# Dilated attention: the two key sets of both heads of a pair joined in one pass, statistics moved by small products, keys loaded once, work moved from VectorE to GpSimd

## The chip, the cores and the metric

The kernel runs on one core of a Trainium2 chip. The metric is the device time of one execution in microseconds (us); three executions gave a median of 2361.89 us (2360.36 to 2362.08). The engines are named as in the profile: PE is TensorE (its weight loads are PEld), DVE is VectorE, ACT is ScalarE, POOL is GpSimd, SP is SyncE, which issues nearly all DMAs here. Each engine works through its own instructions in order; a waiting instruction holds up everything behind it on the same engine.

## The reference, cut to what matters

One encoder layer for 1024 sample rows and 256 prompt rows of width 1024: a half-weighted SwiGLU, a mixer (attention for 512 of the columns, a convolution module for the other 512), a second SwiGLU and a final norm. The change lies within the attention, which has 8 heads of 64 columns and mixes three dilations:

```
DILATED_BRANCHES = ((128, 1), (512, 4), (2048, 16))
for window, dilation in DILATED_BRANCHES:
    o, lse = dilated_branch(q, k, v, slopes, dilation, window // (2 * dilation))
w = softmax(stack(lses), axis=0)
o = sum(w[..., None] * stack(outs), axis=0)
```

Each branch is a softmax over a band of keys at a stride, with a bias that falls linearly with distance; the branches are weighted by their softmax denominators. For the 1024 sample rows the kernel sorts the key/query pairs into two key sets: a first set of 8 blocks of 128 queries that lie 4 rows apart (dilations 4 and 16 together), and a second set of 8 blocks of 128 neighbouring queries (dilation 1). Each set gives an unnormalized output, a minimum and a sum per row; joining the two sets is the step that the change rewrites. The 256 prompt rows have one key set and are only normalized.

## The kernel before

In the span of the profile the stages follow each other: the first SwiGLU to about 910 us, the input projection with the convolution running beside it on the other engines to about 1197, attention to about 1357, the output projection, which starts under the last steps of attention and ends near 1475, then the second SwiGLU.

**Attention** (`attn`, L782 on) goes through `seq`, 8 heads of 9 groups, 72 iterations. Groups 0 to 3 are the first key set of the sample rows, group 4 the prompt rows, groups 5 to 8 the second key set. An iteration issues, in this order: `t_group` for the group of 4 iterations ago (four PE transposes of the probabilities, L943, evacuated from PSUM to `pT` by DVE for groups in `DV_G`, L937, by ACT for the others, L939); `qk_group` for its own group (four products of q with the high and low part of k, L861 and L862, then on DVE the bias and the row minimum into `ast`, L866); small steps by `when(lag, group, step)`; `pv_group` for the group of 6 iterations ago (products with v, L971); `exp_group` (ACT's exponential with the row sum into `ast`, L872). Heads work in pairs: both heads of a pair accumulate into the same two outputs, `oa` and `ob`, which are evacuated after the odd head. A scheduler then lays the instructions of each engine out in one fixed order, near to the order of the code.

**Joining** was done once per head, counted from its last group: `merge1` (16 GpSimd copies of 32 partitions, L892) moves the statistics of the first key set to the rows of the second; `merge2` (three small DVE operations, L900 to L902), `merge3` (ACT's exponential, L905) and `merge4` (DVE, L910 to L915) make two factors for each of 1024 rows; `merge5` turns them by a transpose on PE (`psm`, L920), ACT copies them to `asb` (L922), two DMAs write them to DRAM (`fd`, L925) and two DMAs read them back, spread over 64 partitions (`x`, L932). At lag 10 of the odd head `combine1` multiplies both outputs by them on POOL (L1021). At lag 13 `combine2` adds them: POOL writes the rounded sum `hi` (L1030), DVE the exact sum (L1031) and the remainder `lo` (L1032), the parts that the output projection multiplies.

**Other steps.** `load_qk` loads q twice and both parts of k twice (L808, L810), once for each half of the 128 partitions, since q and k are kept doubled; this is issued two heads ahead. `cast_qb` (L815, POOL) makes a reordered copy of q. `prompt_norm` (L882, DVE) scales the probabilities of the prompt rows. `next_tab` changes the bias tables between heads (L831 on DVE, L833 on POOL).

**DMA queue.** All these DMAs are issued by SP in program order, among them `fd`, `x`, the loads of q, k and v for the head two ahead, and near the end the loads of the weights of the output projection (`raw`, L77; split by ACT, L90, and DVE, L91, into `whi` and `wlo`). Issues that a buffer or an earlier DMA holds up delay those behind them. PSUM has four banks that the score products, transposes and `psm` share in turn, and two double banks for `oa`, `ob` and `pso`.

Of the kernel before, what the change touches and what calls it, by code (L numbers as in the profile page):

```python
# [28 lines left out]
NH = 8  # L29
# [3 lines left out]
NEG = -1e30  # L33
NV = 25
BGA, BGQ, BGV = 9, 4.4, 2.2
DV_G = (1, 4, 7)

# [111 lines left out]
class Trunk:  # L149
# [52 lines left out]

    def rstd(self, src, junk, mul):
        nc = self.nc
        st = self.stp.tile([P, 2], F32, name="st", tag="st", bufs=9)
# [576 lines left out]
    def attn(self, qk, pool, rpool, qd, kd, vd, after):  # L782
# [17 lines left out]
        for i, z in enumerate(tab + [half]):  # L800
            nc.sync.dma_start(z, self.a["tab"][i])

        def load_qk(h):
            d = H.setdefault(h, {})
            q, qb, k, d["v"] = bufs[h % 2]
            f = slice(h * HD, (h + 1) * HD)
            for i in range(2):
                nc.sync.dma_start(q[i * HD:(i + 1) * HD].bitcast(F32), qd[i, f, :])  # L808
            for z, o, s in ((0, 0, 0), (0, HD, 0), (1, 0, 1), (1, HD, 1)):
                nc.sync.dma_start(k[z][o:o + HD, :, 16:16 + 256].bitcast(F32), kd[s, f, :].rearrange("f (c i) -> f c i", c=5))  # L810
            d["q"], d["qb"], d["k"] = q, qb, k

        def cast_qb(h):
            q, qb = bufs[h % 2][0:2]
            nc.gpsimd.tensor_copy(qb.rearrange("p (b c j) -> p b c j", b=8, c=4),  # L815
                                  q[:, 0:NS].rearrange("p (c b j) -> p b c j", b=8, c=4).bitcast(F32))
# [18 lines left out]
        def qk_group(h, g):  # L835
            d = H[h]
            if g == 0:
                d["st"] = self.stp.tile([P, 36], F32, name="ast", tag="ast", bufs=3)
# [39 lines left out]
        def prompt_norm(h):  # L878
            d = H[h]
            nc.vector.reciprocal(d["st"][:, 17:21:2], d["st"][:, 17:21:2])  # L880
            for u in (8, 9):
                nc.vector.tensor_scalar(d["P"][u], d["P"][u], d["st"][:, 2 * u + 1:2 * u + 2], None, op0=OP.mult)  # L882

        def merge1(h):
            d = H[h]
            d["X"] = pool.tile([P, 8, 2], F32, name="ax", tag="ax", bufs=2)
            x = d["X"].rearrange("p (h r) s -> p h r s", h=2)
            for c in range(4):  # L890
                for r in range(4):
                    nc.gpsimd.tensor_copy(x[c * 32:(c + 1) * 32, :, r, :],  # L892
                                          d["st"][r * 32:(r + 1) * 32, 4 * c:4 * c + 4].rearrange("p (h s) -> p h s", s=2))

        def merge2(h):
            d = H[h]
            y = d["y"] = pool.tile([P, 4, 8], F32, name="ay", tag="ay", bufs=2)
            z = d["B"] = d["st"][:, 20:36].rearrange("p (b s) -> p b s", s=2)
            v = nc.vector.tensor_tensor
            v(y[:, 3], d["X"][:, :, 0], z[:, :, 0], op=OP.min)  # L900
            v(y[:, 0], y[:, 3], d["X"][:, :, 0], op=OP.subtract)
# [5 lines left out]
        def merge4(h):  # L907
            d = H[h]
            y, v = d["y"], nc.vector.tensor_tensor
            v(y[:, 2], d["X"][:, :, 1], y[:, 0], op=OP.mult)  # L910
            v(y[:, 3], d["B"][:, :, 1], y[:, 1], op=OP.mult)
            v(y[:, 3], y[:, 2], y[:, 3], op=OP.add)
            nc.vector.reciprocal(y[:, 2], y[:, 3])
            for i in range(2):
                v(y[:, i], y[:, i], y[:, 2], op=OP.mult)  # L915

        def merge5(h):
            d = H[h]
            ps = self.bank("psm")
            nc.tensor.transpose(ps[:16, :P], d["y"].rearrange("p i b -> p (i b)")[:, 0:16], self.ident)  # L920
            sb = pool.tile([16, P], F32, name="asb", tag="asb", bufs=2)
            nc.scalar.activation(sb, ps[:16, :P], AF.Copy)  # L922
            fd = self.dp.tile([2, NS], F32, name=f"fd{h}")
            for i in range(2):
                nc.sync.dma_start(fd[i].rearrange("(c b j) -> b c j", c=4, b=8), sb[8 * i:8 * i + 8].rearrange("b (c j) -> b c j", c=4))  # L925
            if h % 2 == 0:
                d["F"] = [self.tmp("x"), self.tmp("x")]
            else:
                d["F"] = H[h - 1]["F"]
            o = (h % 2) * HD  # L930
            for i in range(2):
                nc.sync.dma_start(d["F"][i][o:o + HD, :], fd[i:i + 1, :].to_broadcast([HD, NS]))  # L932
# [90 lines left out]
        def combine2(h):  # L1023
            d = H[h]
            if h % 2:
                ta, tb = d["t"]
                for t in range(2):
                    c = slice(t * 512, (t + 1) * 512)
                    hi, lo = (z[:, h // 2, :] for z in self.hT[t])
                    nc.gpsimd.tensor_tensor(hi, ta[:, c], tb[:, c], op=OP.add)  # L1030
                    nc.vector.tensor_tensor(ta[:, c], ta[:, c], tb[:, c], op=OP.add)  # L1031
# [5 lines left out]
        load_v(0)  # L1037
        load_qk(1)
        load_v(1)
        cast_qb(0)  # L1040
        cast_qb(1)

        def at(i):
            return seq[i] if 0 <= i < len(seq) else (-1, -1)

        for i in range(len(seq) + LAG + LAG2 + 11):
            def when(k, g, f):
                h, gg = at(i - k)
                if gg == g and h >= 0:
                    f(h)  # L1050

            hq, gq = at(i)
            ht, gt = at(i - LAG)
            hv, gv = at(i - LAG - LAG2)
            if ht >= 0:
                t_group(ht, gt)
            when(5, 8, merge5)
            when(3, 8, merge3)
            if hq >= 0:
                qk_group(hq, gq)  # L1060
            when(2, 4, prompt_norm)
            when(1, 8, merge1)
            when(2, 8, merge2)
            when(4, 8, merge4)
# [12 lines left out]
    def w_out(self, S, base, stages, new_hT):  # L1077
# [253 lines left out]
```

## Time and profile before

| | us |
|---|---|
| median of three executions | 2361.89 |
| the profiled execution's own time | 2361.37 |
| its span | 2359.6 |
| PE busy, whole span | 2288.8 (97%) |
| POOL busy, 1200 to 1380 | 82.16 |
| DVE busy, 1200 to 1380 | 124.73 |
| ACT busy, 1200 to 1380 | 123.68 |
| PE busy, 1200 to 1380 | 163.12 |

PE is the engine that nearly never rests; in the 180 us of attention and the start of the output projection it is idle for 16.9 us in all. A row of the windows view gives a stretch of the span, its length, and for each engine its busy time with its number of instructions; then the TensorE clock that was granted as a share of full speed, the busy share of the DMA engines and GB/s. A row of a timeline gives start, duration, engine, line, operation, output and inputs; in brackets stands how long the engine was idle before it, and what ended that.

### The profile page before, as it was taken

Reading aid. Unit: us, or ns where it says so; the run is one execution under the profiler, and the core shown is the slowest. Engines: PE = TensorE matmul, PEld = TensorE weight load, DVE = VectorE, ACT = ScalarE, POOL = GpSimd, SP = SyncE. Lnnn points to the kernel's source line nnn. Section 1 sums busy time; section 2 is a strip of 40 time slices with the busy share of each in tenths; the row PEclk is TensorE's granted clock in tenths of the full one; section 3 lists DMA queues with packets and bytes.
Section 4 is the critical chain, followed back from the end, with each engine's and each line's share of the span. In section 5 each row is a group of like instructions: output and inputs, shape, how many; then the busy total and the mean of one; then the engine's idle time right before and its main releaser. Section 6 shows DMA issues by size and latency. Waiting matters only on the chain.

```text
span 2359.6 us, 30593 instructions
## 1 busy us (share of the span) xinstructions
PE 2288.8 (97%) x11788; PEld 1959.3 (83%) x11788; DVE 1274.9 (54%) x1796; ACT 808.5 (34%) x1530; POOL 670.3 (28%) x702
## 2 busy tenths in 40 slices
PE   7999999999999999999998999999999999999996
PEld 7888888888788887888887878888888888788885
DVE  5844444344554567998466733834344444545457
ACT  5322222223221224664376722322222222312123
POOL 2332232231000034896125443223233232000004
PEclk9999999999999999999999999999999999999998
DMA  5121221213332333331279642122222222523224
GB/s 161 49 76 59 76 69 61 81 63 112 117 101 78 104 108 125 109 104 50 99 162 180 152 132 96 52 79 63 70 72 63 70 76 77 156 74 94 85 81 154
DMA packets 209240, 223.51 MB, mean 95 GB/s; under 512 B 31012, under 2 KB 161060, under 8 KB 209094
## 3 DMA queue, kind: packets, MB, share of 16 engines
q1 hardware_dynamic: 209094, 221.56, 31.7%
q8 instruction: 92, 1.51, 0.3%
q14 instruction: 54, 0.44, 0.1%
HBM read 163.52 MB, written 58.00 MB: 94 GB/s over the span
## 4 chain that ended last, share of the span: by engine, by line
PE 87%; DVE 4%; DMA 3%; issue 2%; POOL 2%; ACT 2%; SPq 0%; POOLq 0%; ACTq 0%; DVEq 0%
PE psAB L198 8%; PE psAB L199 8%; PE psAB L200 8%; PE psd L198 7%; PE psd L200 7%; PE psd L199 7%; PE psR L199 3%; PE psR L198 3%; PE psR L200 3%; PE psC L198 3%; PE psC L199 3%; PE psC L200 3%; PE psqk L198 2%; PE psqk L199 2%; PE psqk L200 2%
## 5 line engine op out<-in xcount | busy, mean ns | idle before, releaser
L115 DVE TENSOR_TENSOR wb<-raw,wb 128x512 fp32r<-128x512 f32 x240 | 169.3, 707 | 207.6 <-ACT wb L114 202.8
L114 ACT ACTIVATE wb<-raw 128x512 fp32r<-128x512 f32 x240 | 150.6, 629 | 331.3 <-PE psAB L200 137.6
L207 POOL TENSOR_SCALAR st<-st 128x1 f32<-128x1 f32 x70 | 40.7, 581 | 633.8 <-ACT tmp L206 359.3
L198 PE MATMUL psd<-wd,ahl 128*128 128x512 f32 x500 | 197.2, 394 | 7.0 <-ACT y L571 2.1
L451 POOL TENSOR_TENSOR ac<-ac,tmp 128x512 f32<-128x512 f32 x40 | 66.5, 1662 | 465.9 <-DVE tmp L447 443.3
L199 PE MATMUL psd<-wd,ahl 128*128 128x512 f32 x500 | 195.3, 391 | 0.0
L200 PE MATMUL psd<-wd,ahl 128*128 128x512 f32 x500 | 195.1, 390 | 0.0
L536 ACT ACTIVATE ahl<-ar 128x512 fp32r<-128x512 f32 (+1 forms) x132 | 72.8, 556 | 346.3 <-PE psd L200 249.9
L199 PE MATMUL psR<-hT2l,wb 128*128 128x256 f32 x640 | 181.1, 283 | 0.0
L200 PE MATMUL psR<-hT2h,wb 128*128 128x256 f32 x640 | 180.7, 282 | 0.0
L198 PE MATMUL psR<-hT2h,wb 128*128 128x256 f32 x640 | 180.6, 282 | 0.0
L114 ACT ACTIVATE wb<-g 128x512 fp32r<-128x512 f32 x80 | 50.6, 632 | 230.1 <-POOL g L136 95.5
L198 PEld LDWEIGHTS psR<-hT2h,wb 128*128 128x128 f32 x640 | 122.2, 191 | 6.2
L198 PE MATMUL psAB<-hT0h,wb 128*128 128x512 f32 x320 | 125.6, 392 | 0.0
L198 PE MATMUL psC<-hT1h,wb 128*128 128x512 f32 x320 | 125.5, 392 | 0.0
L199 PE MATMUL psC<-hT1l,wb 128*128 128x512 f32 x320 | 125.5, 392 | 0.0
L199 PE MATMUL psAB<-hT0l,wb 128*128 128x512 f32 x320 | 125.5, 392 | 0.0
L199 PEld LDWEIGHTS psR<-hT2l,wb 128*128 128x128 f32 x640 | 122.2, 191 | 3.3
L200 PEld LDWEIGHTS psR<-hT2h,wb 128*128 128x128 f32 x640 | 122.2, 191 | 3.1
L200 PE MATMUL psAB<-hT0h,wb 128*128 128x512 f32 x320 | 124.6, 389 | 0.0
L200 PE MATMUL psC<-hT1h,wb 128*128 128x512 f32 x320 | 124.5, 389 | 0.0
L573 DVE TENSOR_TENSOR y<-y,psd 128x1024 f32<-128x1024 f32 x70 | 85.3, 1218 | 71.5 <-PE psd L200 71.5
(388 smaller groups left out, 6279.6 us busy)
## 6 DMA issues: line engine op xcount, KB each, us to landing
raw<-in_ffn_w_gu_dram SPq DMA_DIRECT2D x88, 512.0 KB
ad<-ac SPq DMA_DIRECT2D x88, 256.0 KB
g<-in_ffn_w_down_dram SPq DMA_DIRECT2D x44, 512.0 KB
ar<-ad SPq DMA_DIRECT2D x88, 256.0 KB
raw<-in_w_in_dram SPq DMA_DIRECT2D x20, 512.0 KB
ar<-ad SPq DMA_DIRECT2D x44, 128.0 KB
ad<-x SPq DMA_DIRECT2D x40, 128.0 KB
x2d<-y SPq DMA_DIRECT2D x10, 512.0 KB
```

The source lines that it names most:

```text
L114: nc.scalar.activation(out[:, 0], src, AF.Copy)
L115: nc.vector.tensor_tensor(out[:, 1], src, out[:, 0].bitcast(F32), op=OP.subtract)
L198: mm(out, lh[0], rh[0], start=first, stop=False, skip_group_check=more)
L199: mm(out, lh[0], rh[1], start=False, stop=False, skip_group_check=more)
L200: mm(out, lh[1], rh[0], start=False, stop=last, skip_group_check=more)
L207: nc.gpsimd.tensor_scalar(st[:, 0:1], st[:, 0:1], 1e-6 / (mul * mul), None, op0=OP.add)
L451: nc.gpsimd.tensor_tensor(a1, a1, q, op=OP.mult)
L536: nc.scalar.activation(hl[0], r, AF.Copy)
L573: nc.vector.tensor_tensor(y[b], y[b], o, op=OP.add)
```

## The change

Four things change, all within `attn` but for one pool size (`st`, 9 to 10 buffers):

- **k once.** `load_qk` loads each part of k into partitions 0 to 63 alone; `double_k`, new, copies it to the other 64 on POOL (one instruction for each part and head, 64 partitions of 5x256). It is issued beside `cast_qb`.
- **Joining once per pair.** The statistics of both heads lie in one tile. `merge0`, new, moves those of the first key set by four products with 0/1 matrices (`sel`, built once on POOL) into PSUM (`psx`); `merge1` is now four DVE copies out of PSUM; `merge2` to `merge4` work on 16 columns in place of 8, once for the odd head. `merge5`, at lag 6 in place of 5, transposes once for the pair, and writes 16 small DMAs `fd` of 2x4x32 (four rows of the loop for each head and output) and four DMAs `x`.
- **Work from DVE to GpSimd.** The two scalings of `prompt_norm`, and the exact sum of `combine2`, now one 128x1024 addition after both `hi`.
- **Times.** The remainders `lo` become `combine3`, at lag 17 (13 for the last head). `combine1` comes at lag 11 (10 for the last head) in place of 10, `combine2` at 14 (13) in place of 13. `DV_G` has four groups in place of three, so one more evacuation of nine goes to DVE.

```diff
-DV_G = (1, 4, 7)
+DV_G = (1, 3, 5, 7)
...
+        sel = pool.tile([P, 4, P], F32, name="sel")
+        for r in range(4):
+            nc.gpsimd.tensor_copy(sel[:, r].rearrange("p (c j) -> p c j", c=4),
+                                  self.ident[:, None, r * 32:(r + 1) * 32].to_broadcast([P, 4, 32]))
...
-            for z, o, s in ((0, 0, 0), (0, HD, 0), (1, 0, 1), (1, HD, 1)):
-                nc.sync.dma_start(k[z][o:o + HD, :, 16:16 + 256].bitcast(F32), kd[s, f, :].rearrange("f (c i) -> f c i", c=5))
+            for z in range(2):
+                nc.sync.dma_start(k[z][0:HD, :, 16:16 + 256].bitcast(F32), kd[z, f, :].rearrange("f (c i) -> f c i", c=5))
...
+        def double_k(h):
+            for z in bufs[h % 2][2]:
+                nc.gpsimd.tensor_copy(z[HD:, :, 16:16 + 256], z[0:HD, :, 16:16 + 256].bitcast(F32))
...
-                nc.vector.tensor_scalar(d["P"][u], d["P"][u], d["st"][:, 2 * u + 1:2 * u + 2], None, op0=OP.mult)
+                nc.gpsimd.tensor_scalar(d["P"][u], d["P"][u], d["st"][:, 2 * u + 1:2 * u + 2], None, op0=OP.mult)
...
+        def merge0(h):
+            d = H[h]
+            d["xp"] = self.bank("psx")[:, 0:128]
+            for r in range(4):
+                mm(d["xp"][:, 32 * r:32 * r + 32], sel[:, r], d["st2"][:, :, 0:16], start=True, stop=True)
...
             for c in range(4):
-                for r in range(4):
-                    nc.gpsimd.tensor_copy(x[c * 32:(c + 1) * 32, :, r, :],
-                                          d["st"][r * 32:(r + 1) * 32, 4 * c:4 * c + 4].rearrange("p (h s) -> p h s", s=2))
+                q = slice(c * 32, (c + 1) * 32)
+                nc.vector.tensor_copy(x[q], z[q, c])
...
-            fd = self.dp.tile([2, NS], F32, name=f"fd{h}")
-            for i in range(2):
-                nc.sync.dma_start(fd[i].rearrange("(c b j) -> b c j", c=4, b=8), sb[8 * i:8 * i + 8].rearrange("b (c j) -> b c j", c=4))
...
-            for i in range(2):
-                nc.sync.dma_start(d["F"][i][o:o + HD, :], fd[i:i + 1, :].to_broadcast([HD, NS]))
+            d["F"] = [self.tmp("x"), self.tmp("x")]
+            for e in range(2):
+                fd = self.dp.tile([2, NS], F32, name=f"fd{h}{e}")
+                for i in range(2):
+                    o = fd[i].rearrange("(c h r j) -> r h c j", c=4, h=2, r=4)
+                    for r in range(4):
+                        q = 16 * i + 8 * e + 2 * r
+                        nc.sync.dma_start(o[r], sb[q:q + 2].rearrange("h (c j) -> h c j", c=4))
+                for i in range(2):
+                    nc.sync.dma_start(d["F"][i][e * HD:(e + 1) * HD, :], fd[i:i + 1, :].to_broadcast([HD, NS]))
...
-                    nc.vector.tensor_tensor(ta[:, c], ta[:, c], tb[:, c], op=OP.add)
+                nc.gpsimd.tensor_tensor(ta, ta, tb, op=OP.add)
+
+        def combine3(h):
+            if h % 2:
+                ta, tb = H[h]["t"]
+                for t in range(2):
+                    c = slice(t * 512, (t + 1) * 512)
+                    hi, lo = (z[:, h // 2, :] for z in self.hT[t])
                     nc.vector.tensor_tensor(lo, ta[:, c], hi.bitcast(F32), op=OP.subtract)
...
-            when(5, 8, merge5)
-            when(3, 8, merge3)
+            odd(3, 3, merge0)
+            odd(6, 8, merge5)
+            odd(3, 8, merge3)
...
-            when(8, 8, lambda h: cast_qb(h + 2) if h + 2 < NH else None)
-            when(13, 8, combine2)
+            when(8, 8, lambda h: (double_k(h + 2), cast_qb(h + 2)) if h + 2 < NH else None)
+            late(14, 13, combine2)
+            late(17, 13, combine3)
...
-            when(10, 8, combine1)
+            late(11, 10, combine1)
```

How the order of the instructions moves is shown at three places. First SP's queue during heads 4 and 5, when the factors of heads 2 and 3, the second pair, are written. Before, around head 3's factors (`fd_10308`), up to the loads for head 6 (`q_9258`, `kH_9260` and `kL_9261` are buffers of the even heads; `v_9272` and `v_9262` those of v):

```order
L823 DMA v_9272<-vd 128x2x64
L825 DMA v_9272<-vd 32x9x64
L925 DMA fd_10308<-asb 8x4x32 x2
L825 DMA v_9272<-vd 32x9x64
L932 DMA x<-fd_10308 64x1024 x2
L825 DMA v_9272<-vd 32x9x64 x2
L808 DMA q_9258<-qd 64x1280 x2
L823 DMA v_9262<-vd 128x2x64 x2
L810 DMA kH_9260<-kd 64x5x256 x2
L810 DMA kL_9261<-kd 64x5x256 x2
```

Now, at the same place (`fd_10257` holds head 2's factors, `fd_10268` head 3's):

```order
L813 DMA q_9258<-qd 64x1280 x2
L835 DMA v_9272<-vd 32x9x64 x3
L952 DMA fd_10257<-asb 2x4x32 x8
L954 DMA x<-fd_10257 64x1024
L952 DMA fd_10268<-asb 2x4x32
L954 DMA x<-fd_10257 64x1024
L952 DMA fd_10268<-asb 2x4x32 x7
L954 DMA x<-fd_10268 64x1024
L835 DMA v_9272<-vd 32x9x64
L954 DMA x<-fd_10268 64x1024
L815 DMA kH_9260<-kd 64x5x256
L815 DMA kL_9261<-kd 64x5x256
```

Four DMAs for head 3 (and four more, a head earlier, for head 2) have become twenty in one run for both. The loads of k for head 6 stand behind all twenty; its q now goes ahead of them.

The second place is POOL at the same pair. Before, from the statistics copies of head 4 (`ax_10440`) to those of head 5 (`tmp_10219` and `tmp_10220` are the two outputs of heads 2 and 3, `x` their factors, `g` a bias table):

```order
L892 COPY ax_10440<-ast_10191 32x2x2 x16
L1021 TENSOR_TENSOR tmp_10220<-tmp_10220,x_10071 128x1024
L1021 TENSOR_TENSOR tmp_10219<-tmp_10219,x_10072 128x1024
L833 TENSOR_SCALAR g_9279<-g_9279 128x768
L815 CAST qb0_9259<-q0_9258 128x1024
L1030 TENSOR_TENSOR hT0h_9218<-tmp_10219,tmp_10220 128x512
L1030 TENSOR_TENSOR hT1h_9220<-tmp_10219,tmp_10220 128x512
L892 COPY ax_10686<-ast_10431 32x2x2 x16
```

Now (the outputs are `tmp_10146` and `tmp_10147`):

```order
L825 CAST qb0_9259<-q0_9258 128x1024
L843 TENSOR_SCALAR g_9279<-g_9279 128x768
L1043 TENSOR_TENSOR tmp_10147<-tmp_10147,x_10255 128x1024
L1043 TENSOR_TENSOR tmp_10146<-tmp_10146,x_10256 128x1024
L821 CAST kH0_9260<-kH0_9260 64x5x256
L821 CAST kL0_9261<-kL0_9261 64x5x256
L1052 TENSOR_TENSOR hT0h_9218<-tmp_10146,tmp_10147 128x512
L1052 TENSOR_TENSOR hT1h_9220<-tmp_10146,tmp_10147 128x512
L896 TENSOR_SCALAR pr_10462<-pr_10462,ast_10135 128x256 x2
L1053 TENSOR_TENSOR tmp_10146<-tmp_10146,tmp_10147 128x1024
```

The 16 copies per head are gone; between and behind the multiplications stand the doubling of k for head 6 (L821) and, behind those and the additions, the scaling of head 5's prompt probabilities (L896). In the pair before this one L896 stands ahead of L1052; in the pair after it there is no L821.

The third place is the end of SP's queue in attention, behind the last pair's factors. Before:

```order
L77 DMA raw<-in_w_out_dram 128x1024 x4
L925 DMA fd_11240<-asb 8x4x32 x2
L932 DMA x<-fd_11240 64x1024 x2
L77 DMA raw<-in_ffn_w_gu_dram 128x8x128 x2
L77 DMA raw<-in_w_out_dram 128x1024
```

Now:

```order
L77 DMA raw<-in_w_out_dram 128x1024 x4
L952 DMA fd_11115<-asb 2x4x32 x8
L954 DMA x<-fd_11115 64x1024
L952 DMA fd_11126<-asb 2x4x32
L954 DMA x<-fd_11115 64x1024
L952 DMA fd_11126<-asb 2x4x32 x7
L954 DMA x<-fd_11126 64x1024 x2
L77 DMA raw<-in_ffn_w_gu_dram 128x8x128 x2
L77 DMA raw<-in_w_out_dram 128x1024
```

The last of the eight weight loads of the output projection keeps its place behind the factors, whose DMAs have gone from 4 to 20.

More of the change, by code (lines that the diff above doesn't have):

```diff
@@ L204, in rstd @@
         nc = self.nc
-        st = self.stp.tile([P, 2], F32, name="st", tag="st", bufs=9)
+        st = self.stp.tile([P, 2], F32, name="st", tag="st", bufs=10)
         nc.scalar.activation(junk, src, AF.Square, scale=D ** -0.5 / mul, accum_out=st[:, 0:1])
@@ L837, in qk_group @@
             if g == 0:
-                d["st"] = self.stp.tile([P, 36], F32, name="ast", tag="ast", bufs=3)
+                if h % 2 == 0:
+                    d["st2"] = self.stp.tile([P, 2, 36], F32, name="ast", tag="ast", bufs=2)
+                else:
+                    d["st2"] = H[h - 1]["st2"]
+                d["st"] = d["st2"][:, h % 2]
                 d["P"] = {}
@@ L909, in merge4 @@
             y, v = d["y"], nc.vector.tensor_tensor
-            v(y[:, 2], d["X"][:, :, 1], y[:, 0], op=OP.mult)
-            v(y[:, 3], d["B"][:, :, 1], y[:, 1], op=OP.mult)
+            v(y[:, 2], d["X"][:, :, :, :, 1], y[:, 0], op=OP.mult)
+            v(y[:, 3], d["B"][:, :, :, :, 1], y[:, 1], op=OP.mult)
             v(y[:, 3], y[:, 2], y[:, 3], op=OP.add)
@@ L919, in merge5 @@
             ps = self.bank("psm")
-            nc.tensor.transpose(ps[:16, :P], d["y"].rearrange("p i b -> p (i b)")[:, 0:16], self.ident)
-            sb = pool.tile([16, P], F32, name="asb", tag="asb", bufs=2)
-            nc.scalar.activation(sb, ps[:16, :P], AF.Copy)
-            fd = self.dp.tile([2, NS], F32, name=f"fd{h}")
-            for i in range(2):
[L925 to L930, printed above, removed]
-            for i in range(2):
-                nc.sync.dma_start(d["F"][i][o:o + HD, :], fd[i:i + 1, :].to_broadcast([HD, NS]))
+            nc.tensor.transpose(ps[:32, :P], d["y"].rearrange("p i e r h -> p (i e r h)")[:, 0:32], self.ident)
+            sb = pool.tile([32, P], F32, name="asb", tag="asb", bufs=1)
+            nc.scalar.activation(sb, ps[:32, :P], AF.Copy)
+            d["F"] = [self.tmp("x"), self.tmp("x")]
[8 more added lines that the diff above has]
+                    nc.sync.dma_start(d["F"][i][e * HD:(e + 1) * HD, :], fd[i:i + 1, :].to_broadcast([HD, NS]))
         def evac(g, ps):
@@ L1039, in attn @@
         load_v(1)
+        double_k(0)
         cast_qb(0)
+        double_k(1)
         cast_qb(1)
@@ L1050, in when, with late, odd @@
                     f(h)
+            def late(k, k_last, f):
+                for lag, hs in ((k, range(NH - 1)), (k_last, (NH - 1,))):
+                    h, gg = at(i - lag)
+                    if gg == 8 and h in hs:
+                        f(h)
+            def odd(k, g, f):
+                when(k, g, lambda h: f(h) if h % 2 else None)
             hq, gq = at(i)
@@ L1061, in attn @@
             when(2, 4, prompt_norm)
-            when(1, 8, merge1)
-            when(2, 8, merge2)
-            when(4, 8, merge4)
-            when(8, 8, lambda h: cast_qb(h + 2) if h + 2 < NH else None)
-            when(13, 8, combine2)
+            odd(3, 3, merge1)
+            odd(2, 8, merge2)
+            odd(4, 8, merge4)
+            when(8, 8, lambda h: (double_k(h + 2), cast_qb(h + 2)) if h + 2 < NH else None)
+            late(14, 13, combine2)
+            late(17, 13, combine3)
             if hv >= 0:
```

15 lines of the change are left out of this document (8 added, 7 removed).

## Prediction
> **What bounds the kernel now.** I read the page's busy times first, then the windows by head, then the timelines of PE, DVE and POOL at the places where PE stood still, and last the chain of waits at the end of attention.
>
> ```profile
> span 2359.6 us, 30593 instructions
> PE 2288.8 (97%) x11788; PEld 1959.3 (83%) x11788; DVE 1274.9 (54%) x1796; ACT 808.5 (34%) x1530; POOL 670.3 (28%) x702
> 1200.00:1380.00 180.00, 163.12 (x993) 145.26 (x994) 124.73 (x458) 123.68 (x384) 82.16 (x161) 0.94 0.80 172
> ```
>
> PE is the bound of the whole; the only stage that the change touches leaves PE 16.9 us idle in 180 (last row: PE, PEld, DVE, ACT, POOL). By head, each row from the first score product of one head to that of the next (heads 1, 2, 3, 5, 7, the last cut at its last group):
>
> ```profile
> 1213.93:1232.39 18.46, 16.70 (x119) 15.42 (x118) 12.83 (x58) 13.75 (x48) 7.11 (x19) 1.00 1.02 183
> 1232.39:1248.62 16.23, 16.23 (x117) 15.06 (x115) 11.85 (x54) 14.77 (x48) 6.67 (x18) 1.00 1.00 193
> 1248.62:1272.38 23.76, 18.65 (x114) 17.03 (x112) 13.65 (x54) 12.14 (x40) 14.94 (x22) 0.86 0.87 169
> 1289.96:1310.52 20.56, 17.94 (x114) 16.03 (x112) 15.95 (x54) 12.43 (x41) 12.02 (x22) 0.92 0.83 160
> 1327.80:1346.16 18.36, 16.28 (x105) 14.84 (x104) 14.35 (x53) 11.61 (x41) 11.76 (x21) 0.91 0.39 122
> ```
>
> Head 2 is all PE, 16.23 us, 1.80 for each of 9 groups. Heads 3, 5 and 7, in which the outputs of the pair before are combined, are 7.5, 4.3 and 3.9 us longer (the last against 8 groups, 14.4). In each PE stands once, and then runs at a lower clock for a while (0.86, 0.92 and 0.91 in their rows):
>
> ```profile
> 1216.49 0.39 PE L862 MATMUL pss<-kL,q 128*128 128x256 f32 x1 [1.76 <-DMA kL<-kd]
> 1264.92 0.58 PE L861 MATMUL pss<-kH,qb 128*128 128x256 f32 x1 [5.11 <-DVE ast L866]
> 1293.97 1.91 PE L971 MATMUL op<-pT,v 128*128 128x256 f32 x4 [2.26 <-ACT pT L939]
> 1331.62 2.02 PE L971 MATMUL op<-pT,v 128*128 128x256 f32 x4 [2.08 <-ACT pT L939]
> 1263.40:1270.30 6.90, 5.38 (x19) 4.84 (x20) 6.90 (x24) 4.35 (x14) 4.96 (x17) 0.51 0.63 128
> ```
>
> The first row is head 1's. The last is the 6.9 us behind the gap of head 3: the granted clock is 0.51. The causes stand on DVE and POOL:
>
> ```profile
> 1253.41 4.70 POOL L1021 TENSOR_TENSOR to<-to,x 128x1024 f32<-128x1024 f32 x2 [7.68 <-DMA x<-fd]
> 1262.45 1.73 DVE L1031 TENSOR_TENSOR to<-to 128x512 f32<-128x512 f32 x1 [6.79 <-POOL hT0h L1030]
> 1288.39 4.69 POOL L1021 TENSOR_TENSOR tmp<-tmp,x 128x1024 f32<-128x1024 f32 x2 [5.36 <-issue]
> 1290.83 2.28 DVE L901 TENSOR_TENSOR ay<-ay,ax 128x8 f32<-128x8 f32 x1
> 1328.48 2.28 DVE L901 TENSOR_TENSOR ay<-ay,ax 128x8 f32<-128x8 f32 x1
> ```
>
> In head 3 DVE's exact sum stands in DVE's queue waiting 6.79 us for POOL, with the next row minima behind it. In heads 5 and 7 a DVE operation on 8 columns takes 2.28 us beside POOL's multiplication; ACT's exponential of the joining waits for it, the evacuation of `pT` behind that, and PE for `pT`.
>
> **What the change takes away.** The exact sum leaves DVE, and the joining comes once a pair, after odd heads, while the multiplications come a head later: the three collisions go. I take the excess of the three heads, 7.5 + 4.3 + 3.9 = 15.7 us, and of head 1's wait for `kL` half, 0.8, since k's DMAs are halved but a POOL copy follows. **−16.5 us** (−20 with all of head 1's excess and some more, −10 where half of head 3's excess and a third of the others' stays as a smaller wait).
>
> **What it adds on PE.** Before: one transpose a head. Now, a pair: four products with `sel`, each with a weight load, and one transpose less. No row shows such products; four transposes of 128 columns take 0.44, 0.11 each:
>
> ```profile
> 1219.77 0.44 PE pst L943 x4
> L971 PEld LDWEIGHTS oa<-pT,v 128*128 128x128 f32 x160 | 27.5, 201 | 2.7
> L892 POOL COPY ax<-ast 32x4 f32<-32x4 f32 x128 | 29.7, 232 | 13.7 <-ACT pr L872 8.8
> ```
>
> Eight instructions by 0.11, less 0.11, is 0.77 a pair, **+3.1** for four; from 0 (hidden in what idle time stays) to 6.4 (eight by the 201 ns of a weight load).
>
> **What it adds beside PE.** POOL loses 128 copies (29.7 us, the row above) and gains, by these rows,
>
> ```profile
> L815 POOL CAST qb<-q 128x1024 fp32r<-128x1024 f32 x7 | 7.3, 1037 | 29.8 <-DMA q<-qd 29.8
> L833 POOL TENSOR_SCALAR g<-g 128x768 f32<-128x768 f32 x7 | 15.0, 2137 | 7.4 <-DVE ast L866 7.4
> L1030 POOL TENSOR_TENSOR hT0h<-to 128x512 fp32r<-128x512 f32 x2 | 2.6, 1276 | 0.0
> L937 DVE COPY pT<-pst 128x512 f32<-128x512 f32 x24 | 16.5, 686 | 5.9 <-PE pst L943 5.9
> L882 DVE TENSOR_SCALAR pr<-pr,ast 128x256 f32<-128x256 f32 x16 | 4.9, 348 | 0.0
> ```
>
> 16 doublings of k at 1.3 (1037 ns by 1280 for 1024 elements) = 20.8, 16 scalings at 0.71 (2137 by 256 for 768) = 11.4, and 4 sums at 2.35 (half of 4.70) = 9.4: 12 us more, 94 of 180. DVE loses 4.9 and gains 8 evacuations, 5.5. Both have room in the mean, so their sums cost nothing; what counts is where POOL's queue is late, since scaling and doubling are now waited for by PE.
>
> For that, a table by hand, from the last score product of the odd head (t = 0):
>
> ```profile
> 1309.71 0.36 PE L861 MATMUL pss<-kH,qb 128*128 128x256 f32 x1
> 1320.85 0.63 SPq L925 DMA_DIRECT2D fd<-asb  x2
> 1358.77 0.64 SPq L925 DMA_DIRECT2D fd<-asb  x2
> 1360.33 1.09 SPq L932 DMA_DIRECT2D x<-fd  x2
> 1364.47 4.75 POOL L1021 TENSOR_TENSOR tmp<-tmp,x 128x1024 f32<-128x1024 f32 x2 [23.00 <-DMA x<-fd]
> ```
>
> The first `fd` was issued 11.1 after it (head 5: 1309.71 to 1320.85), now a group later, 12.9. Then SP issues 16 `fd` at 0.32 (5.1), four `x` at 0.55 (2.2), with one landing between, 0.9 (1358.77 + 0.64 to 1360.33), and the last lands 3.05 later (1360.33 + 1.09 to 1364.47): 24.2. POOL: two multiplications, 28.9; in the second pair two doublings of k, 31.5; two `hi`, 34.1; two scalings, 35.5; the sum, 37.9. The transposes that need the scaled prompt group come 18 groups after t = 0, at 32.4: **3.1 late**. DVE's `lo` is in its queue at about 36 there, in head 6's first group, and waits till 37.9; I count 1.5. The doubled k is in time (31.5 for 34.2). In the first pair the scaling stands ahead of `hi`, in the third no k is doubled: 24.2 + 4.7 + 2.6 + 1.4 = 32.9 in both, 0.5 late each, 1.0; and one collision of a small DVE operation with a POOL sum, 2.3 by the 2.28 rows. **+8** (0 to 14).
>
> A row bears on those collisions:
>
> ```profile
> 1293.05 2.13 POOL L833 TENSOR_SCALAR g<-g 128x768 f32<-128x768 f32 x1
> 1293.79 0.15 DVE L910 TENSOR_TENSOR ay<-ax,ay 128x8 f32<-128x8 f32 x1
> ```
>
> POOL's one-input scaling ran over a two-input DVE operation that still took 0.15, so the 2.28 belongs to POOL's two-input operations, which the change has in `hi`, sum and multiplication; the 32 scalings and doublings are left out. The Trainium skill, page "SBUF — State Buffer", section "Who interferes with whom", says that a DVE instruction with two SBUF inputs and any GpSimd instruction that reads SBUF shut each other out. L901 agrees with it, L910 doesn't; by the rule the new one-input instructions would hold DVE too, and the sum be as in the third rival below.
>
> The doublings of heads 0 and 1 fall into the end of the input projection, where POOL is busy 37.3 of 40 us:
>
> ```profile
> 970.00:1010.00 40.00, 40.00 (x200) 34.08 (x199) 36.83 (x36) 24.97 (x46) 37.28 (x38) 1.00 0.51 149
> ```
>
> This is the densest stretch of that stage; q and k of head 0 come at its end, and PE has products of its own till then. **0** (−1 to +4, three of the four doublings ahead of the first score product).
>
> **The end of attention.** There the chain of waits runs through a DMA:
>
> ```profile
> 1362.78 8.62 DMA raw<-in_w_out_dram
> ...
> 1372.51 1.24 DVE wlo L91
> 1373.79 0.50 PE pso L199
> 1346.16:1376.36 30.20, 30.07 (x147) 24.72 (x145) 16.84 (x28) 15.91 (x27) 7.28 (x4) 1.00 0.66 202
> ```
>
> The last weights of the output projection are issued right behind the pair's factors and two other loads, and PE, fully busy until then (30.07 of 30.20), gets them just in time. The 14 more `fd` and two more `x` push this issue back by 14 × 0.32 + 2 × 0.55 = 5.6, and the transpose a group later by about 0.5: PE would stand some 6 us, and the clock drop behind it, as after the other gaps, adds 1.4. **+7.5** (4, if the weights land two or three us sooner, to 9).
>
> **Sum.** −16.5 + 3.1 + 8 + 0 + 7.5 = +2.1 on the profiled execution's own 2361.37 (span 2359.6; the median of the runs is 0.5 above it): **2363.5 us**. The bounds of the terms that most decide, +8 and +7.5, give 2352 to 2371.
>
> **Rivals.** (1) *The new waits stay away.* `fd` may be issued earlier, and PE can go on with other groups when the scaling is late, as no row of before shows PE waiting for POOL directly. Against it: POOL's queue is in order and the table has it 3 us late. With +2 for the waits and +4 at the end: −16.5 + 3.1 + 2 + 4 = −7.4, 2354. (2) *The factors are late in all pairs*, slower. SP's twenty DMAs follow each other in time only if none waits for an earlier one; if one or two landings of up to 3 us come between, with the DMA engines 0.83 to 1.00 busy as in the rows of heads 2, 3 and 5, the factors come 4 us later, at 28.2. POOL's multiplications hold its queue meanwhile, with scaling and doubling behind, and by the table none of the three pairs has slack: 3 × 4 = +12, 2375.5. It decides from factors later than 24 on, by 3 us for each. (3) *POOL still holds DVE*: if its scalings and doublings also shut out DVE's small operations, half of what heads 3, 5 and 7 lost, 8 us, comes back: 2371. The rule of the skill's page above would bring this one about.
>
> **Chances.** Forecast 0.43, of which 0.37 within 0.2%, the rest split; rival 1 0.28; rival 2 0.18; rival 3 0.07; anything else 0.04. About 4.7 us (0.2%) is what a measurement of this kernel can tell from no change. So faster 0.32, same 0.38, slower 0.30. The range goes from just below rival 1 to just above rival 2, 2350 to 2377; the forecast's own is 2356 to 2369.
>
> **What would show it.** Heads 3, 5 and 7 near 17 us, no 2 us DVE operation on 16 columns, and no DVE wait for `hi`: the −16.5. PE waiting for POOL's L896 in head 5: the table. SP's `fd` issues over 0.32 each or `x` landing later than 24 us after the odd head's last product: rival 2. PE idle some 6 us before the last `wlo` at about 1365 to 1372 of the new span: the end. It is wrong if the weights come no later, or if a PE wait for row minima is left in head 3.

## The result, and the profile after

The changed kernel takes **2386.81 us** (median of 5, 2384.58 to 2388.93), the kernel before 2361.89 beside it: a ratio of 1.0115, 95% interval 1.0102 to 1.0129, slower by some 25 us. The forecast was 2363.5, its range 2350 to 2377.

First the page of the changed kernel, its span and busy times:

```profile
span 2387.1 us, 30597 instructions
PE 2311.3 (97%) x11816; PEld 1959.8 (82%) x11816; DVE 1266.8 (53%) x1760; ACT 805.6 (34%) x1514; POOL 693.8 (29%) x614
```

The span is 27.5 us longer, and PE is 22.5 us busier, although only 28 more of its instructions are recorded. Next the windows view: of the kernel before, from the first score product to the last group of head 7, from there to the last product of the output projection, 40 us in the middle of the second down projection, which the change doesn't touch, and heads 4 and 6:

```profile
1197.46:1346.16 148.70, 133.32 (x857) 120.84 (x856) 109.15 (x433) 110.31 (x363) 74.99 (x156) 0.93 0.85 171
1346.16:1473.54 127.38, 124.91 (x587) 103.67 (x586) 49.42 (x60) 41.87 (x74) 44.48 (x49) 0.99 0.36 121
2160.00:2200.00 40.00, 40.00 (x178) 33.14 (x177) 20.78 (x22) 7.88 (x12) 0.00 (x0) 1.00 0.29 90
1272.38:1289.96 17.58, 17.20 (x120) 15.36 (x117) 13.39 (x58) 15.76 (x54) 7.55 (x19) 1.00 0.95 180
1310.52:1327.80 17.28, 17.09 (x120) 15.40 (x117) 13.84 (x58) 15.24 (x53) 7.72 (x19) 1.00 0.90 170
```

and of the changed kernel: attention, its heads 2 to 6, the end of attention with the output projection, and the same 40 us:

```profile
1203.52:1352.50 148.98, 136.12 (x883) 121.74 (x881) 102.35 (x395) 106.56 (x346) 85.73 (x65) 0.94 0.66 139
1239.65:1257.41 17.76, 16.94 (x116) 15.03 (x115) 12.48 (x53) 13.86 (x46) 7.47 (x7) 1.00 0.47 96
1257.41:1275.46 18.05, 17.45 (x124) 15.78 (x122) 11.79 (x48) 13.44 (x43) 12.88 (x9) 1.00 0.85 172
1275.46:1296.30 20.84, 18.52 (x117) 16.27 (x115) 15.12 (x55) 13.59 (x45) 12.21 (x10) 0.92 0.48 90
1296.30:1316.51 20.21, 17.57 (x124) 15.83 (x121) 11.30 (x48) 13.21 (x43) 15.35 (x11) 1.00 0.88 166
1316.51:1336.98 20.47, 18.75 (x116) 16.92 (x115) 15.54 (x55) 13.94 (x45) 9.54 (x7) 0.83 0.27 63
1352.50:1488.19 135.69, 127.16 (x589) 104.10 (x588) 48.13 (x62) 42.15 (x74) 50.50 (x51) 0.99 0.35 116
2160.00:2200.00 40.00, 40.00 (x173) 32.19 (x172) 18.80 (x21) 7.48 (x11) 0.00 (x0) 1.00 0.27 83
```

Four things are to be seen. Attention as a whole is as long as before (148.98 for 148.70): heads 3 and 7 are 5.7 and 2.8 us shorter, but heads 2, 4 and 6 are 1.5 to 3.3 longer. The end of attention with the output projection is 8.3 longer. Attention begins 6.1 us later, and what follows the output projection takes 898.9 in place of 886.1, 12.8 more. So 18.9 us are lost in stages whose code is the same. There, in the last row, PE is busy all the time at full clock, but does 173 products in 40 us where it did 178. The groups of one shape tell which products are slower (mean ns of one after the comma), before:

```profile
L199 PE MATMUL psd<-wd,ahl 128*128 128x512 f32 x500 | 195.3, 391 | 0.0
L198 PE MATMUL psAB<-T2h,wb 128*128 128x512 f32 x160 | 62.3, 389 | 0.0
L199 PE MATMUL psd<-wdh0h,ahl 128*128 128x512 f32 x120 | 46.7, 389 | 0.0
```

and after:

```profile
L199 PE MATMUL psd<-wd,ahl 128*128 128x512 f32 x500 | 198.0, 396 | 0.0
L198 PE MATMUL psAB<-T2h,wb 128*128 128x512 f32 x160 | 63.1, 394 | 0.0
L199 PE MATMUL psd<-wdh0h,ahl 128*128 128x512 f32 x120 | 46.7, 389 | 0.0
```

Products with `wd` and `T2` (and `T3`, `T4`) take 5 ns more each, those with `wdh0h` nothing. `wdh0h` lies in SBUF ahead of the pool of small statistics, whose size the change alters (`st` 9 to 10 buffers, `ast` 3 of 144 bytes to 2 of 288); the others lie behind it (but for four tiles of `wd` at the other end of SBUF), and in the built program they stand 128 bytes higher than before (`T2h` at 125280 in place of 125152 in each partition). 1440 products with T and 1500 with `wd`, at 5 ns, are 15 us of the 18.9. In the trace such a product starts 227 ns after the last one before, 232 after (medians).

Inside attention, the waits of PE in the changed kernel (total, times, longest):

```profile
PE pss L875 <- DVE ast L880: 4.7, 3, 2.2
PE pst L965 <- POOL pr L896: 4.6, 3, 2.6
PE pso L199 <- DVE wlo L91: 4.5, 2, 4.0
PE pso L198 <- DVE tmp L212: 3.1, 1, 3.1
```

The second is the wait for POOL's scaling that the prediction's table had: 2.59 us of it in head 5 and 0.55 in head 3. The remaining 1.43 stands at the end of head 0, before any factors are written, so late factors aren't its cause. For the second pair SP issued the first `fd` 16.5 us after the last group of head 3 began (1274.54), by SP's timeline:

```profile
1291.06 3.60 SPq L952 DMA_DIRECT2D fd<-asb  x8
```

and POOL's timeline from there is:

```profile
1304.03 5.44 POOL L1043 TENSOR_TENSOR tmp<-tmp,x 128x1024 f32<-128x1024 f32 x2 [4.72 <-DMA x<-fd]
1309.53 1.25 POOL L821 CAST kH<-kH 64x1280 fp32r<-64x1280 f32 x1
1310.72 1.25 POOL L821 CAST kL<-kL 64x1280 fp32r<-64x1280 f32 x1
1312.06 1.27 POOL L1052 TENSOR_TENSOR hT0h<-tmp 128x512 fp32r<-128x512 f32 x1
1313.29 1.26 POOL L1052 TENSOR_TENSOR hT1h<-tmp 128x512 fp32r<-128x512 f32 x1
1314.53 1.82 POOL L896 TENSOR_SCALAR pr<-pr,ast 128x256 f32<-128x256 f32 x2
1316.32 2.36 POOL L1053 TENSOR_TENSOR tmp<-tmp 128x1024 f32<-128x1024 f32 x1
1318.62 1.04 POOL L825 CAST qb<-q 128x1024 fp32r<-128x1024 f32 x1
1319.63 2.15 POOL L843 TENSOR_SCALAR g<-g 128x768 f32<-128x768 f32 x1
1321.84 1.25 POOL L821 CAST kH<-kH 64x1280 fp32r<-64x1280 f32 x1
```

DVE's joining of the next pair falls beside the end of this work (DVE's timeline of the same time):

```profile
1317.16 1.56 DVE L922 TENSOR_TENSOR ay<-ax,ast 128x16 f32<-128x16 f32 x1
1318.76 0.94 DVE L923 TENSOR_TENSOR ay<-ay,ax 128x16 f32<-128x16 f32 x1
1319.62 0.17 DVE L924 TENSOR_TENSOR ay<-ay,ast 128x16 f32<-128x16 f32 x1
1322.37 0.75 DVE L934 TENSOR_TENSOR ay<-ay 128x16 f32<-128x16 f32 x1
```

L922 ends as POOL's sum L1053 ends, L923 as the cast of q ends, L934 as the doubling of k ends; L924 takes its 0.17, but it started together with the one-input L843. At the start of head 4 it is POOL's `hi` additions and the cast of q that hold L923 for 1.18 us and L924 for 1.06. L843 holds such an operation too, if only in its first part: at the start of head 2, L923 began 0.11 us into L843 (1240.64) and took 0.76. The kernel before shows the same:

```profile
1277.11 2.13 POOL L833 TENSOR_SCALAR g<-g 128x768 f32<-128x768 f32 x1
1277.27 0.68 DVE L912 TENSOR_TENSOR ay<-ay 128x8 f32<-128x8 f32 x1
```

L912 ended 0.84 us after L833 had begun. In the profiles of all runs, 40 of these small operations began 0.08 to 0.68 us into a 128x768 TENSOR_SCALAR; every one ended 0.84 to 0.89 us after its start, and those that began 0.7 to 2.0 us into it took 0.15 to 0.19.

At the end of attention, DVE's timeline shows a wait that the prediction didn't have:

```profile
1376.42 3.50 DVE L91 TENSOR_TENSOR wlo<-raw,whi 128x1024 fp32r<-128x1024 f32 x3 [12.84 <-DMA fd<-asb]
1386.94 1.28 DVE L91 TENSOR_TENSOR wlo<-raw,whi 128x1024 fp32r<-128x1024 f32 x1 [7.02 <-ACT whi L90]
```

The remainder of the fifth unit of weights is held up for 12.84 us by the DMAs that read `asb`: in the built program its tile (225248 to 229344) takes over the bytes of `asb` (228832), and may be written only when all 16 `fd` have read them.

### The profile page after: what moved, and what is told of

The parts are those of the page before. It is cut to its first block, busy times and chain, and to the rows that moved or that the text cites. A ratio compares the mean times of both kernels' runs of the same rounds, so it can differ in the third digit from the quotient of the medians.

```text
span 2387.1 us, 30597 instructions
## 1 busy us (share of the span) xinstructions
PE 2311.3 (97%) x11816; PEld 1959.8 (82%) x11816; DVE 1266.8 (53%) x1760; ACT 805.6 (34%) x1514; POOL 693.8 (29%) x614
## 4 chain that ended last, share of the span: by engine, by line
PE 84%; DVE 4%; DMA 4%; POOL 3%; issue 2%; ACT 1%; SPq 1%; POOLq 0%; ACTq 0%; DVEq 0%
PE psAB L198 8%; PE psAB L200 8%; PE psAB L199 8%; PE psd L198 7%; PE psd L199 7%; PE psd L200 7%; PE psR L198 3%; PE psR L199 3%; PE psR L200 3%; PE psC L199 3%; PE psC L198 3%; PE psC L200 3%; PE psqk L198 2%; PE psqk L200 2%; PE psqk L199 2%
## 5 line engine op out<-in xcount | busy, mean ns | idle before, releaser
L198 PE MATMUL psd<-wd,ahl 128*128 128x512 f32 x500 | 199.6, 399 | 7.1 <-ACT y L571 2.4
L199 PE MATMUL psd<-wd,ahl 128*128 128x512 f32 x500 | 198.0, 396 | 0.0
L200 PE MATMUL psd<-wd,ahl 128*128 128x512 f32 x500 | 197.9, 396 | 0.0
```

Of the source, the lines that this page charges most:

```text
L198: mm(out, lh[0], rh[0], start=first, stop=False, skip_group_check=more)
L199: mm(out, lh[0], rh[1], start=False, stop=False, skip_group_check=more)
L200: mm(out, lh[1], rh[0], start=False, stop=last, skip_group_check=more)
```

## The experiments

**Is it the place in SBUF? (e1 to e4).** In the kernel before, unused bytes are put into the pool of small statistics (n = 32 floats for e1, 16 for e2), with one `asb` buffer to make room. In the changed kernel the same with n = 32 (e3) and 96 (e4), room being made by one `ay` buffer, in e4 one `ax` buffer too:

```diff
-        self.stp = ctx.enter_context(tc.tile_pool(name="stp", bufs=4))
+        self.stp = ctx.enter_context(tc.tile_pool(name="stp", bufs=4)); self.stp.tile([P, n], F32, name="pad", tag="pad", bufs=1)
```

> The kernel before with 128 unused bytes per partition in the pool of small statistics (and one asb buffer in place of two to make room), so that every SBUF tile allocated behind that pool lies 128 bytes higher, as in the changed kernel. Layout theory: products whose moving operand is T2, T3, T4 or wd go from 227 ns start to start (389 to 393 ns mean length) to about 232 (395), and the time rises by 15 to 20 us, to about 2379. Rival (the slowdown outside attention comes from the changed instructions themselves): these products stay at 227 ns and the time within 5 us of 2362.

> The kernel before with 64 unused bytes in the same pool (asb one buffer). Layout theory with a period above 64 bytes: the same products get slower, by 5 ns each if any address off the old one does it, or stay at 227 ns if only some offsets do; time 2362 to 2380. Rival: 227 ns, within 5 us of 2362.

> The changed kernel with 128 unused bytes in the same pool (and one ay buffer to make room), so that the tiles behind it lie 256 bytes higher than before. Layout theory with a period of 256 bytes: T2, T3, T4 and wd products back at 227 ns, time 15 to 19 us below the changed kernel, 2368 to 2372. Layout theory with a longer period, or the rival: 232 ns and 2387.

> The changed kernel with 384 unused bytes in the same pool (one ay and one ax buffer), tiles 512 bytes higher than before. Layout theory with a period of 256 or 512 bytes: 227 ns and 2368 to 2372. Rival: 232 ns and 2387.

Measured: e1 2380.27 (one run), e2 2370.65 (one run), e3 2371.96 (ratio to before 1.0051, 1.0036 to 1.0066), e4 2370.39 (1.0047, 1.0029 to 1.0066); before, on the same chip, 2359.68. The windows row of e1, with nothing changed but these bytes and the `asb` buffer (e12 below has one `asb` buffer too, and is fast), is that of the changed kernel:

```profile
2160.00:2200.00 40.00, 40.00 (x173) 32.17 (x172) 19.55 (x21) 7.89 (x12) 0.00 (x0) 1.00 0.27 82
```

and that of e4, the changed kernel with 384 more, that of the kernel before:

```profile
2160.00:2200.00 40.00, 40.00 (x178) 33.14 (x177) 20.52 (x22) 7.34 (x12) 0.00 (x0) 1.00 0.29 89
```

Medians from start to start for `T2h`: 232 ns in e1, 231 in e2, 227 in e3 and e4. The layout theory holds, with a period of 256 bytes: 64 and 128 bytes are bad, 256 and 512 good. 64 costs about half as much: of the three products that belong together, the first takes 232 ns there, the second (`T2l`) 226 as before, the third 229, and the time rose by 11 us where it rose by 20.6 in e1. In the changed kernel the layout is worth 2386.8 − 2370.4 = 16 us of the 25. What is left, some 11 us over the kernel before on the same chip, is the change's own doing, and e4 is the base for the next.

**Which of the two operands? (e8, e12).** e8 lowers the other end of SBUF, with the stationary and streamed weights, by 128 bytes; e12 does that and raises all the rest by 128 as well (both with one `asb` buffer):

```diff
+    self.ctx.enter_context(tc.tile_pool(name="padr", bufs=1, side="right")).tile([P, 32], F32, name="padr")
     wp, wp_x = pool_("wp", bufs=9, side="right")
...
+        self.const.tile([P, 32], F32, name="padl")   # e12 only
         self.hp = ctx.enter_context(tc.tile_pool(name="hp", bufs=1))
```

> The kernel before with the tiles of the other end of SBUF (wb, ahl, part of wd, the stationary and streamed weights) 128 bytes lower, and T2 to T4 and hT0 to hT2 where they were. If it is the distance between the moving and the stationary operand that counts: products of T2 to T4 and of hT0 and hT1 with wb go from 227 to 232 ns, time 2380 or more. If it is the place of the moving operand alone: T and hT products stay at 227 ns, only those with wd on that side slow down, time 2362 to 2370.

> The kernel before with both ends of SBUF moved: hT, T and the left part of wd 128 bytes higher (96 in place of 224 modulo 256), wb and ahl 128 bytes lower (also 96 in place of 224). Theory that the distance between moving and stationary operand modulo 256 decides: it is 0 again, products at 226 to 227 ns, time within 5 us of before. Rival (224 is a good place and 96 a bad one, for either operand): 232 ns or more and 2380 or more.

e8: 2389.43 (one run), no faster than the changed kernel; now the products with `wdh0h` are slow as well, though that tile hasn't moved (e8's group):

```profile
L199 PE MATMUL psd<-wdh0h,ahl 128*128 128x512 f32 x120 | 47.3, 394 | 0.0
```

e12: 2356.22 (0.9992, 0.9983 to 1.0002), with `T2h` at 389 ns again. Neither operand's own place counts, but the **distance of the two modulo 256 bytes**: 0 is fast. (All tiles of weights leave the same remainder, so no run tells the weights in use from those that are loaded beside the product.) In the kernel before it happened to be 0 for nearly all products of these stages (T from 125152 and `wb` from 184288 both leave 224).

**What of the change costs the other 11 us? (e5, e6, e7, e9, e13).** All on the base of e4. e5 lays the columns of the factors out by head, set and row, so that one DMA takes 8 rows of `asb`:

```diff
-            y = d["y"] = pool.tile([P, 4, 2, 4, 2], F32, name="ay", tag="ay", bufs=1)
+            d["yr"] = pool.tile([P, 4, 2, 2, 4], F32, name="ay", tag="ay", bufs=1)
+            y = d["y"] = d["yr"].rearrange("p i e h r -> p i e r h")
...
-                    for r in range(4):
-                        q = 16 * i + 8 * e + 2 * r
-                        nc.sync.dma_start(o[r], sb[q:q + 2].rearrange("h (c j) -> h c j", c=4))
+                    q = 16 * i + 8 * e
+                    nc.sync.dma_start(fd[i].rearrange("(c b j) -> b c j", c=4, b=8), sb[q:q + 8].rearrange("b (c j) -> b c j", c=4))
```

e6 puts the scaling of `prompt_norm` back on DVE; e7 takes `double_k` out and loads k by the four DMAs of before; e9 is e5 and e7 together; e13 is e5 with the doubling on ACT:

```diff
-                nc.gpsimd.tensor_scalar(d["P"][u], ...)   # e6
+                nc.vector.tensor_scalar(d["P"][u], ...)
...
-                nc.gpsimd.tensor_copy(z[HD:, :, 16:16 + 256], z[0:HD, :, 16:16 + 256].bitcast(F32))   # e13
+                nc.scalar.activation(z[HD:, :, 16:16 + 256], z[0:HD, :, 16:16 + 256].bitcast(F32), AF.Copy)
```

> The kernel of e4 (changed kernel, tiles 512 bytes higher than before) with the factors laid out so that 4 DMAs fd in place of 16 write them for a pair. Theory: the 12 DMAs less give SP's queue back 12 x 0.3 = 3.7 us for each pair, the last weights of the output projection are issued and PE's wait for wlo (4.2 us in e4) falls to under 1, and the factors reach POOL 3 to 4 us earlier: 4 to 8 us below e4, 2362 to 2366. Rival (the time is lost to POOL's work holding DVE and PE, wherever the DMAs stand): within 2 us of e4's 2370.

> The kernel of e4 with the two scalings of prompt_norm back on DVE. Theory: PE's waits for POOL's scaling (2.9 us in e4) go and POOL is 14 us less busy, so its sums come earlier and collide less with the joining: 3 to 6 us below e4, 2364 to 2367. Rival: DVE pays with 4.9 us of its own and the waits move to the row minima: within 2 us of 2370.

> The kernel of e4 with k loaded in four DMAs a head again and no doubling on POOL. Theory: POOL is 20 us less busy and its sums come 2.5 us earlier in the first two pairs, SP has two DMAs more a head (1.1 us): 1 to 4 us below e4, 2366 to 2369. Rival (loading once pays, since DMA traffic holds the factors up): 1 to 4 us above e4.

> The kernel of e4 with both k in four DMAs (as e7) and the factors in four DMAs (as e5). Theory (the doubling on POOL costs attention 8 us, the 20 DMAs of the factors cost the end 4 us): attention as in e7, 141 us from first to last score product, PE's wait for wlo under 2, time 2 to 5 us below e7: 2358 to 2361, the same as before. Rival (with k's DMAs back SP is late and the factors come no earlier): 2363.

> The kernel of e5 (k loaded once, factors in four DMAs) with the doubling of k on ACT in place of POOL. Theory (the doubling costs because POOL's queue stands for k's DMA and for the 1.25 us of each copy, with the scaling and the sums behind it): most of the 11 us between e5 and e9 comes back, 2357 to 2362. Rival (it costs because k arrives later or because of the reads themselves): within 2 us of e5's 2368. ACT pays 2.5 us a head, and if ACT's queue stands for the DMA in turn, it is slower than e5.

| | us (median) | ratio to before, interval |
|---|---|---|
| e4, base | 2370.39 | 1.0047 (1.0029 to 1.0066) |
| e5, four `fd` | 2367.76 | 1.0039 (1.0026 to 1.0052) |
| e6, scaling on DVE | 2373.11 | 1.0062 (1.0049 to 1.0075) |
| e7, k in four DMAs | 2363.17 | 1.0021 (1.0011 to 1.0031) |
| e9, e5 and e7 | 2356.29 | 0.9992 (0.9982 to 1.0001) |
| e13, e5 with doubling on ACT | 2373.37 | 1.0072 (1.0059 to 1.0086) |

The windows of attention, first score product to head 7's last group, one kernel each: e4, e7, e9.

```profile
1195.86:1344.96 149.10, 136.46 (x882) 121.06 (x881) 105.04 (x395) 106.23 (x346) 85.93 (x65) 0.95 0.64 139
```

```profile
1196.27:1336.93 140.66, 132.32 (x882) 120.27 (x881) 103.18 (x395) 106.50 (x346) 65.43 (x49) 0.96 0.86 179
```

```profile
1194.55:1331.85 137.30, 129.64 (x882) 118.93 (x881) 99.61 (x394) 106.26 (x343) 71.08 (x51) 0.98 0.88 184
```

The runs come from several chips, so the ratios are what can be compared. Loading k once makes attention 8.4 us longer (149.10 for 140.66): the largest single cost within the change. The small DMAs cost less than expected beside it, 2.6 us, which the overlapping intervals of e4 and e5 don't tell from nothing, though PE's longest wait for `wlo` fell from 4.2 to 0.8 us; without the loading once they cost 6.9 (2363.17 to 2356.29). With both undone, attention is 11.4 us shorter than before, so the joining by pairs does there what it was reckoned to do. The whole is no faster all the same. The end of attention with the output projection takes 132.4 us in e9, for 127.4 before:

```profile
1331.85:1464.25 132.40, 126.49 (x587) 103.76 (x588) 53.71 (x63) 42.72 (x78) 49.74 (x50) 0.99 0.35 119
```

PE waits there 3.1 us for `tmp` (2.3 before) and 2.0 for `wlo` (none before); no run takes the rest apart, nor the 3.8 us that the unchanged stages behind it took longer in this profile. e6's theory fell: with the scaling on DVE the time is 2.7 us above e4, not below (the intervals overlap), so nothing shows this part of the change as the culprit. e13 fell too: on ACT the doubling is dearer still. ACT's group and PE's waits in e13 say why:

```profile
L821 ACT ACTIVATE kH<-kH 64x1280 fp32r<-64x1280 f32 x7 | 8.9, 1269 | 14.2 <-DMA kH<-kd 14.2
```

```profile
PE pss L875 <- ACT pT L960: 5.4, 7, 1.5
PE pst L964 <- ACT pT L960: 4.0, 2, 3.7
```

ACT stood 14.2 us for k's DMA and 17.8 in copying (kL took as long as kH), with the evacuations that PE needs behind it. So it isn't POOL alone; on ACT the cost is a copy that is waited for on an engine with work for PE behind it. How much of the 8.4 us on POOL is its copies' own time (14 of 1.25 us in attention, 17.5) and how much that they shut out DVE's two-input operations isn't told apart.

**The doubling alone (e10).** The kernel before, its own layout, with `load_qk` and `double_k` as in the change and nothing else of it.

> The kernel before (its own layout) with k loaded once and doubled on POOL, and nothing else of the change. Theory that the doubling costs by itself: 3 to 8 us above before, attention longer by as much. Rival (it costs only where POOL also has the scaling and the sum): within 2 us of before, or below it, since head 1's wait for kL of 1.8 us goes.

2369.74 us (1.0044, 1.0032 to 1.0057): 11 us slower, above what was expected. Attention takes 156.57 us (148.70 before), and PE has a new wait, 8.1 us in all:

```profile
PE psm L924 <- DVE ay L919: 8.1, 5, 2.9
```

There POOL's copies of the statistics stand behind the doublings, the joining behind them, and its transpose, an instruction of 0.37 us whose result the multiplications need only five groups later, holds all of PE.

**The end of attention (e11, e14, e15).** e11 is e9 with the last pair's exact sum on DVE; e14 is e11, and e15 is e4, with `asb` in the pool of small statistics (and the unused bytes chosen so that the tiles behind stand 768 higher, 0 modulo 256):

```diff
-                nc.gpsimd.tensor_tensor(ta, ta, tb, op=OP.add)
+                (nc.vector if h == NH - 1 else nc.gpsimd).tensor_tensor(ta, ta, tb, op=OP.add)   # e11, e14
...
-            sb = pool.tile([32, P], F32, name="asb", tag="asb", bufs=1)
+            sb = self.stp.tile([32, P], F32, name="asb", tag="asb", bufs=1)   # e14, e15
```

> The kernel of e9 with the exact sum of the last pair back on DVE, since in e5 POOL's sum of 3.3 us stood ahead of the small POOL step that the output projection's first result waits for. Theory: that step comes 3 us earlier and PE's wait for tmp (3.1 us in e5) falls to under 1: 1 to 3 us below e9, 2356 to 2359. Rival: DVE's two sums of 0.95 us delay its lo and its own next steps as much: within 1 us of e9.

> The kernel of e11 with asb in the pool of small statistics (tiles behind it 768 bytes higher than before, 0 modulo 256). In e4, e5 and e9 DVE's wlo of the fifth weight unit stood 9 to 13 us for the DMAs fd, since its tile takes the bytes of asb. Theory: this wait goes, wlo follows whi by about a microsecond, PE's waits for wlo (3.3 us in e11) fall under 1, and the time is 2 to 6 us below e11: 2350 to 2354, faster than before. Rival (the last weights are late anyway, as their DMA stands behind the factors): within 1.5 us of e11.

> The kernel of e4 with asb in the pool of small statistics, all else as e4. Theory (PE's 4.2 us for wlo in e4 come from the reuse of asb's bytes): that wait goes, but the last weights, still issued behind 20 DMAs, are waited for later, 1 to 4 us; time 1 to 4 us below e4: 2366 to 2369. Rival (the 4.2 us come from the late issue alone): the wait stays at 4 us, time within 1 us of e4.

e11: 2355.86 (0.9992, 0.9983 to 1.0001), no different from e9. Its theory fell: PE's wait for `tmp` went from 3.1 to 2.4 us, not under 1, and that for `wlo` rose from 2.0 to 3.3. e15: 2373.46 (1.0059, 1.0046 to 1.0072), not faster than e4. Its waits of PE at the end show that the wait for `wlo` went and another of the same size came:

```profile
PE pso L198 <- ACT whi L90: 4.0, 1, 4.0
PE pso L198 <- DVE tmp L212: 3.6, 1, 3.6
PE pso L199 <- DVE wlo L91: 0.6, 1, 0.6
```

`whi` waits for the last weights themselves, issued behind the 20 DMAs. Both causes end at the same time here, so that taking one away gains nothing; the theory that the reuse of `asb`'s bytes alone made the 4 us fell. e14: 2355.95 (0.9985, 0.9976 to 0.9993), the only version whose interval lies below before, by 0.15%; its median is that of e11, so the 2 to 6 us that were expected of it didn't come.

## Why the prediction was wrong, step by step

- **The step that failed first** is the frame of the sum, "the only stage that the change touches": the stages outside attention and its end were taken to keep their time, without a reason. They took 18.9 us longer in the profile. The shift of 128 bytes, from a change of 128 bytes in a pool of small tiles, slowed 2940 unchanged products by 5 ns. Its price is 16 us (e4 against the changed kernel), and no term or rival had it. Without it the kernel takes 2370.4, within the range, and 10.7 more than the kernel before on the same chip, where the sum had +2.1.
- **"Both have room in the mean, so their sums cost nothing"** was the second: the 16 doublings, 20.8 us on POOL, were put at nothing beside the table. They cost 7 us as part of the change (e7), 11 with the factors in four DMAs (e5 to e9) and 11 alone (e10).
- **−16.5 from the three collisions** was the right mechanism: with doubling and small DMAs out of the way attention is 11.4 us shorter (e9), and −16.5 + 3.1 is −13.4. In the changed kernel it was given back: heads 4 and 6 take 20.8 and 20.5 us in place of 17.6 and 17.3, since POOL's additions and casts for the pair before now come late enough to meet the next joining (`hi` in head 4, the exact sum in head 6); with doubling and small DMAs out of the way (e9) they take 17.6 and 17.0.
- **+3.1 for the products with `sel`** came out about right, in part by luck: eight products are recorded for a pair, 0.81 us from start to start, 3.2 for four, where the sum had counted four products and four weight loads.
- **+8 for the new waits.** The mechanism was right: PE waited 2.59 us for POOL's scaling in head 5, where the table had 3.1, though a scaling took 0.92 us in place of its 0.71. The table itself was 5 us early: `fd` was issued after 16.5 us, not 12.9, and the multiplications began after 29.5 (1304.03), not 24.2. That is rival 2's delay, but PE, late itself by then, waited for the scaling only 3.1 us behind the factors (heads 3 and 5).
- **Scalings and doublings "left out" as holders of DVE.** Wrong, and rival 3 in part: L923 and L934 end with the casts beside them, and a 128x768 TENSOR_SCALAR holds such an operation for its first 0.85 us. The row that this was judged by, L910, began 0.74 us into L833, when the hold was all but over; L912, beside L833 a head earlier, took 0.68 and was overlooked. The rule on the shared port ("SBUF — State Buffer", "Who interferes with whom", in the Trainium skill) agrees with the casts, the two-input sums and the first 0.85 us of a TENSOR_SCALAR, not with its other 1.3 us. How much time these holds cost in all isn't told apart from the rest.
- **+7.5 at the end**: measured 8.3 (135.69 for 127.38), the size in part by luck. PE waited 4.05 us for weights, not 6, and first for another reason than predicted; e15 shows that the predicted one would have cost as much. A part that wasn't reckoned is POOL's sum of 3.3 us for the last pair, ahead of the small POOL step behind PE's wait of 3.1 us for `tmp`; moving it to DVE (e11) brought 0.7 us there, and nothing in the time.
- **0 for the input projection** was right: in e4, which has the doublings but not the shift, attention begins at 1195.86, no later than before (1197.46).

## What to carry to other kernels

A change of some bytes in a small pool moves every tile behind it: compare the addresses of the operands of the main products before and after, and look at the count of products in a stage that the change doesn't touch before any of its steps is blamed. A copy put on an engine that is half idle costs its place in that engine's queue: look what stands behind it that PE waits for, and what it stands behind itself. And where two waits end together, taking away one shows nothing until the other goes too.

## What the runs showed of the hardware

PE's rate on 128x512 products depends on the distance in SBUF between the moving operand and the weights: 226 to 227 ns from start to start at 0 modulo 256 bytes, 231 to 232 at 128 (e1, e8 and the changed kernel), and 232, 226 and 229 in turn at 64 (e2). PE was busy all the time at granted clock 1.00 in all of them, in the 40 us from 2160. No run tried other distances or says what makes PE wait; products of 256 columns stayed at 118 to 120 ns in e8, where their operands lie 128 bytes apart as well. A GpSimd cast holds a small two-input DVE operation until it ends (0.94 and 0.75 us for 0.17); a GpSimd TENSOR_SCALAR of 2.13 us holds it only for its first 0.85.
